# Second score product of the attention at 128 rows, the residual's post-norm weights under an ordering hint, and another buffer for the SGU mix

## The chip, the cores and the metric

One Trainium2 chip, one of its cores. The metric is the time of one execution on the device, in microseconds (us), as the median of several runs. The engines are named as in the profile: PE is the matrix engine (PEld its weight loads), DVE the vector engine, ACT the scalar engine, POOL is GpSimd, SP issues most transfers.

## The reference

Batch 1, 256 latent tokens and 256 context tokens, width 1024, float32. Two "trunk" layers come first, then one block with a forgetting attention, an LRU and a mixture of 32 experts, which the change does not touch. A trunk layer, cut to what matters (the attention has 8 query heads of 64, 2 key heads and 512 keys; layer 0 does the same for the context, over its own 256 keys):

```python
def trunk_layer(x, ctx, c, c_ctx, p, ang_r, ang_c, need_ctx):
    ...
    (a_q, a_k, a_v, a_g, g_q, g_k, g_v, g_af, g_ab, g_g,
     s_u, s_v, s_g, m_a, m_g, m_s) = jnp.split(h @ p['w_in'], pts, axis=-1)
    ...
    y_attn = blocked_attention(ql, k_all, v_all) * jax.nn.silu(a_g)
    ...
    y_gla = gla_finish(ol_f + flip(ol_b), p['gla_o_norm'], x.dtype) * jax.nn.silu(g_g)
    y_sgu = sgu(s_u, s_v, p['sgu_ln_g'], p['sgu_ln_b'], p['sgu_w'], p['sgu_b']) * jax.nn.silu(s_g)
    def merge(ya, yg, ys, ga, gg, gs):
        m = (jax.nn.sigmoid(ga) * (ya @ p['w_br_attn'])
             + jax.nn.sigmoid(gg) * (yg @ p['w_br_gla'])
             + jax.nn.sigmoid(gs) * (ys @ p['w_br_sgu']))
        return m @ p['w_out']
    out = merge(y_attn, y_gla, y_sgu, m_a, m_g, m_s)
    x_new = layer_norm(DEEPNORM_ALPHA * x + gate[:, None, :] * out, p['post_g'], p['post_b'])
    ...
```

## The kernel before, in words

Float32 products are made from a high and a low part of each operand: a product of activations `hTh`, `hTl` with weights `whi`, `wlo` is three matmuls (L228, L229, L230; or L263 to L265). The weights stream from HBM (`raw`), ACT makes the high part (L97) and DVE the low part (L98).

Each trunk layer has three branches that need only its input: attention (`attn_core`), a gated linear attention (GLA, `gla_pair`, two pairs of heads), and the SGU (`sgu_core`). The `merge` then multiplies a gate (`mgps`, three per chunk of columns) with each branch's projection (`brps<-ysg`, `brps<-ygl`, and of the attention) and adds them into `msum`. Layer 0 carries 512 tokens, layer 1 only the 256 latent ones.

The attention takes 128 tokens at a time (`tt`: four in layer 0, two in layer 1). The first two see 512 keys, the last two of layer 0 see 256. For each of four query heads `r` there are two key heads `g`; I call one (`r`, `g`) a head. Its scores are two products into one PSUM tile `asc`: L609 takes all 128 rows (64 rows are the high part of the query, 64 its low part; the high part of the keys, `kh`, stands in both halves of the partitions), and L611 takes 64 rows (the query's high part by the keys' low part `kl`). DVE takes the maximum (L616), ACT the exponential (L619), DVE the sum's reciprocal and the scaling (L620, L621), PE transposes (`trp`, L624), ACT evicts (L626), and PE multiplies by the values into one half of the columns (`aops`, L631). At the end of a `tt`, DVE multiplies by the gate and splits (L635, L637). The SGU multiplies on PE (`mxps`), DVE adds (L917, it empties a PSUM buffer of tag "gm", which the gates `mgps` use too), POOL multiplies (L920), ACT and DVE split (L922).

The order of instructions is not written out: a scheduler at build time walks the program with its own model of the engines and fixes each engine's list. On the chip each engine works through its list in order. A tile's buffer is handed to the next tile of the same tag, which then waits for the old one's readers; the list order follows these waits. `tc.issue_after(i)` adds an ordering edge, without a wait, from instruction `i` to instructions of the same engine.

After layer 1's branches, the residual `x2` (two tiles of 128x1024) is multiplied by a post-norm weight and a bias is added, on POOL (L1132, L1133); the weight comes by a transfer (`post<-post_ln_g`).

Of the kernel before, what the change touches and what calls it, by code (L numbers as in the profile page):

```python
# [10 lines left out]
F32 = mybir.dt.float32  # L11
F32R = mybir.dt.float32r
# [3 lines left out]
OP = mybir.AluOpType  # L16
# [59 lines left out]
class Builder:  # L76
# [409 lines left out]
    def attn_tiles(self):  # L486
        L = self.L
        a1 = self.slot.tile([128, 2, 4, self.nx], F32, tag=self.half, bufs=self.nhalf, name="a1")
        L["a1"] = a1
        L["qT"], L["agT"] = a1[:, 0], a1[:, 1]  # L490

        L["kh"] = self.akv.tile([128, 2, 512], F32R, tag="kh", name="kh")
        L["kl"] = self.akv.tile([128, 512], F32R, tag="kl", name="kl")
        L["v"] = self.akv.tile([128, 4, 128], F32, tag="v", name="v")

    def attn_kv(self, t0, t1):
        nc, a, L = self.nc, self.a, self.L
        kh, kl, v = L["kh"], L["kl"], L["v"]
        tts = range(t0 // 128, t1 // 128)
        g = self.gemm_tok(self.chunk(a["w_in"][self.li], C_AK), tts)  # L500
        for tt in tts:
            kt = self.att.tile([128, 512], F32, tag="att2k", name="ktok")[:, :128]
            nc.scalar.activation(v[:, tt], g[tt][:, 128:256], AF.Copy)
            self.norm_rope(g[tt][:, 0:128], 2, 1, tt, kt.rearrange("p (h e) -> p h e", e=64))
            ps = self.ptr.tile([128, 128], F32, tag="tr", name="trk")
            nc.tensor.transpose(ps, kt, self.ident)
            ts = slice(tt * 128, tt * 128 + 128)
            for h in range(2):
                pr, other = slice(64 * h, 64 * h + 64), slice(64 - 64 * h, 128 - 64 * h)
                nc.scalar.activation(kh[pr, h, ts], ps[pr], AF.Copy)  # L510
                nc.vector.tensor_tensor(kl[pr, ts], ps[pr], kh[pr, h, ts].bitcast(F32), op=OP.subtract)
                nc.gpsimd.tensor_copy(kh[other, h, ts], kh[pr, h, ts])

    def attn_q(self):
        nc, a, L = self.nc, self.a, self.L
        w = a["w_in"][self.li]
        nq = self.nx // 128
        a1, qT = L["a1"], L["qT"]
        qtok = {}
        for c in range(2):  # L520
            g = self.gemm_tok(self.chunk(w, C_AQ + 256 * c), range(nq))
            for tt in range(nq):
                if c == 0:
                    qtok[tt] = a1[:, 1].rearrange("p r t -> p (r t)")[:, 512 * tt:512 * tt + 512].rearrange(
                        "p (r g e) -> p r g e", r=4, g=2)
                self.norm_rope(g[tt], 4, 0, tt, qtok[tt][:, :, c])
        for tt in range(nq):
            ps = self.ptr.tile([128, 4, 128], F32, tag="tr", name="trq")
            for r in range(4):
                nc.tensor.transpose(ps[:, r], qtok[tt][:, r].rearrange("p g e -> p (g e)"), self.ident)  # L530
            nc.scalar.activation(qT[:, :, tt * 128:tt * 128 + 128], ps, AF.Copy)
# [57 lines left out]
    def attn_core(self):  # L589
        nc, L = self.nc, self.L  # L590
        nq = self.nx // 128
        qT, kh, kl, v = L["qT"], L["kh"], L["kl"], L["v"]
        halves = [slice(64 * g, 64 * g + 64) for g in range(2)]
        y = L["y_a"] = self.slot.tile([128, 2, 4, self.nx], F32R, tag="slot", name="yat")
        for tt in range(nq):
            keys = (0, 512) if tt < 2 else (256, 512)
            nk = keys[1] - keys[0]
            nkc = nk // 128
            ops = self.pou.tile([128, 4, 128], F32, tag="ou", name="aops")

            qs = self.att.tile([128, 4, 2, 128], F32R, tag="qs", name="qs")
            for g in range(2):
                src, hi = qT[halves[g], :, tt * 128:tt * 128 + 128], qs[halves[g], :, g]
                nc.scalar.activation(hi, src, AF.Copy)
                nc.vector.tensor_tensor(qs[halves[1 - g], :, g], src, hi.bitcast(F32), op=OP.subtract)
            for r in range(4):
                sc = [self.psc.tile([128, 512], F32, tag="sc", name="asc")[:, :nk] for g in range(2)]
                for g in range(2):
                    nc.tensor.matmul(sc[g], qs[:, r, g], kh[:, g, keys[0]:keys[1]], start=True, stop=False)  # L609
                for g in range(2):  # L610
                    nc.tensor.matmul(sc[g], qs[halves[g], r, g], kl[halves[g], keys[0]:keys[1]], start=False, stop=True)  # L611
                pts = []
                for g in range(2):
                    s = sc[g]
                    st = self.sm.tile([128, 4], F32, tag="ast", name="ast")
                    nc.vector.tensor_reduce(st[:, 0:1], s, axis=AX.X, op=OP.max)  # L616
                    nc.vector.tensor_scalar(st[:, 1:2], st[:, 0:1], -0.125, None, op0=OP.mult)
                    p = self.att.tile([128, 512], F32, tag="att2k", name="p")[:, :nk]
                    nc.scalar.activation(p, s, AF.Exp, scale=0.125, bias=st[:, 1:2], accum_out=st[:, 2:3])  # L619
                    nc.vector.reciprocal(st[:, 3:4], st[:, 2:3])  # L620
                    nc.vector.tensor_scalar(p, p, st[:, 3:4], None, op0=OP.mult)  # L621
                    tp = self.ptr.tile([128, 4, 128], F32, tag="tr", name="trp")
                    for k in range(nkc):
                        nc.tensor.transpose(tp[:, k], p[:, k * 128:k * 128 + 128], self.ident)  # L624
                    pt = self.att.tile([128, 4, 128], F32, tag="pt", bufs=2, name="pt")
                    nc.scalar.activation(pt[:, :nkc], tp[:, :nkc], AF.Copy)  # L626
                    pts.append(pt)

                for k in range(nkc):
                    for g in range(2):  # L630
                        nc.tensor.matmul(ops[halves[g], r], v[:, keys[0] // 128 + k, 64 * g:64 * g + 64], pts[g][:, k],  # L631
                                         start=(k == 0), stop=(k == nkc - 1), skip_group_check=True)
            t = self.tmp.tile([128, 4, 128], F32, tag="tmp", name="yt")
            tc = slice(tt * 128, tt * 128 + 128)
            nc.vector.scalar_tensor_tensor(t, ops, 0.5, L["agT"][:, :, tc], op0=OP.mult, op1=OP.mult)  # L635
            nc.scalar.activation(y[:, 0, :, tc], t, AF.Copy)
            nc.vector.tensor_tensor(y[:, 1, :, tc], t, y[:, 0, :, tc].bitcast(F32), op=OP.subtract)  # L637


    def gla_tiles(self):  # L640
# [266 lines left out]
    def sgu_core(self):  # L907
        nc, L = self.nc, self.L
        y = L["y_s"]
        for tt in range(self.nx // 128):  # L910
            ps = self.pgm.tile([128, 4, 128], F32, tag="gm", name="mxps")
            for g in range(4):
                nc.tensor.matmul(ps[:, g], L["vn"][:, tt, g * 128:g * 128 + 128], L["wsT"][:, g], start=True, stop=True,
                                 skip_group_check=True)
            t = self.att.tile([128, 4, 128], F32, tag="mx", bufs=1, name="mx")
            for g in range(4):
                nc.vector.scalar_tensor_tensor(t[:, g], ps[:, g], L["vT"][:, 28 + g:29 + g], L["sgr"][:, g],  # L917
                                               op0=OP.mult, op1=OP.add)
            tc = slice(tt * 128, tt * 128 + 128)
            nc.gpsimd.tensor_tensor(t, t, L["su"][:, :, tc], op=OP.mult)  # L920
            nc.scalar.activation(y[:, 0, :, tc], t, AF.Copy)
            nc.vector.tensor_tensor(y[:, 1, :, tc], t, y[:, 0, :, tc].bitcast(F32), op=OP.subtract)  # L922
# [101 lines left out]
    def first_block(self):  # L1024
        nc, tc, a = self.nc, self.tc, self.a
        with ExitStack() as st:
# [15 lines left out]
            with ExitStack() as layer:  # L1042
# [47 lines left out]
                with ExitStack() as inner:  # L1090
                    self.merge_pools(inner)
                    self.xp = self.pool("xp", side="right", reuse_waits="tile")
                    x2 = self.xp.tile([128, 2, D], F32, tag="x", bufs=1, name="x2")
# [25 lines left out]
            with ExitStack() as layer:  # L1119
# [6 lines left out]
                with ExitStack() as inner:  # L1126
# [2 lines left out]
                    self.h2T = [h2p.tile([128, 8, 256], F32R, name=n) for n in ("h2Th", "h2Tl")]  # L1129
                    pv = self.post_norm(0)  # L1130
                    for t in range(2):
                        nc.gpsimd.tensor_tensor(x2[:, t], x2[:, t], pv[:, 0], op=OP.mult)  # L1132
                        nc.gpsimd.tensor_tensor(x2[:, t], x2[:, t], pv[:, 1], op=OP.add)  # L1133
                    pv = self.post_norm(1)
                    side = self.pool("lru", side="right", stack=self.right, reuse_waits="tile")
                    self.merge(iter(()))
# [25 lines left out]
                    ps = self.psc.tile([128, 512], F32, tag="sc", name="rmps")  # L1162
# [808 lines left out]
```

## Time and profile before

| | before |
|---|---|
| median of 3 runs | 1340.52 us (1338.68 to 1343.06) |
| the profiled execution | 1342.17 us, span 1339.8 us |
| mean granted PE clock | 0.981 of full speed |
| PE busy | 1262.4 us, 94% of the span |
| DVE, ACT, POOL busy | 724.2, 577.9, 334.9 us |

The span is the profiled stretch on the core; the remaining 2.4 us of the execution lie outside it. Layer 0's attention scores run from 258.6 us on, layer 1's end at 869.4 us. A clock of 1.00 in a row is 2.4 GHz, 0.50 is 1.2 GHz.

### The profile page before, as it was taken

The numbers are of one execution on the slowest core, as the hardware profiler recorded it, in microseconds if no ns is written. First come the engines' busy times: TensorE is split into PE (matmuls) and PEld (weight loads), VectorE is DVE, ScalarE is ACT, GpSimd is POOL, SyncE is SP. The second block draws the span as 40 slices with busy tenths as digits, with TensorE's granted clock in tenths as the row PEclk, the third lists the DMA queues.
The fourth block names the chain that finished last, engine by engine and source line by source line (L and its number), as shares of the span: only waits on it lengthen the run. The fifth ranks groups of instructions, "written<-read, shape, count | busy, mean of one in ns | idle before, by whom it ended". The sixth has DMA issues, their size and how long they took to land.

```text
span 1339.8 us, 22959 instructions
## 1 busy us (share of the span) xinstructions
PE 1262.4 (94%) x8819; PEld 977.2 (73%) x8819; DVE 724.2 (54%) x1428; ACT 577.9 (43%) x1115; POOL 334.9 (25%) x373
## 2 busy tenths in 40 slices
PE   6999999999999999999999999999899989999975
PEld 3789888777777766799989988799898675333311
DVE  2565585775443323378768877646878455111112
ACT  2463454455343222346776554545465333222201
POOL 2237645340001101242246545002124020000000
PEclk9999999999999999999999999999899799999998
DMA  9613222211124676545555546246498546999994
GB/s 320 188 53 110 74 58 79 65 48 48 48 75 132 188 252 221 173 149 167 152 149 157 138 116 186 67 126 193 123 327 252 187 174 257 409 408 409 408 409 185
DMA packets 182165, 243.89 MB, mean 182 GB/s; under 512 B 15284, under 2 KB 154780, under 8 KB 182048
## 3 DMA queue, kind: packets, MB, share of 16 engines
q1 hardware_dynamic: 182048, 242.35, 54.9%
q8 instruction: 71, 1.16, 0.4%
q14 instruction: 46, 0.38, 0.1%
HBM read 241.27 MB, written 1.05 MB: 181 GB/s over the span
## 4 chain that ended last, share of the span: by engine, by line
PE 65%; DMA 15%; DVE 8%; ACT 4%; issue 3%; POOL 2%; SPq 1%; ACTq 0%; DVEq 0%; POOLq 0%
DMA gu<-w_up 7%; PE mgps L228 5%; PE mgps L230 5%; PE mgps L229 5%; PE gmt L263 4%; PE gmt L264 4%; PE gmt L265 4%; PE gups L1737 3%; DVE wlo L98 2%; DMA dn<-w_down 2%; DMA raw<-w_in 2%; PE brps L228 2%; PE brps L229 2%; PE brps L230 2%; PE aops L631 2%
## 5 line engine op out<-in xcount | busy, mean ns | idle before, releaser
L98 DVE TENSOR_TENSOR wlo<-raw,whi 128x1024 fp32r<-128x1024 f32 (+1 forms) x202 | 253.5, 1261 | 156.7 <-ACT whi L97 153.8
L97 ACT ACTIVATE whi<-raw 128x1024 fp32r<-128x1024 f32 (+1 forms) x216 | 212.5, 993 | 199.3 <-PE mgps L229 41.8
L264 PE MATMUL gmt<-wlo,hTh 128*128 128x256 f32 x480 | 138.0, 288 | 2.5 <-DVE wlo L98 2.5
L263 PE MATMUL gmt<-whi,hTh 128*128 128x256 f32 x480 | 137.3, 287 | 2.1 <-DVE a L587 0.9
L265 PE MATMUL gmt<-whi,hTl 128*128 128x256 f32 x480 | 137.3, 286 | 0.0
L228 PE MATMUL mgps<-hTh,whi 128*128 128x512 f32 (+1 forms) x384 | 132.0, 345 | 0.0
L229 PE MATMUL mgps<-hTl,whi 128*128 128x512 f32 (+1 forms) x384 | 130.6, 340 | 0.0
L230 PE MATMUL mgps<-hTh,wlo 128*128 128x512 f32 (+1 forms) x384 | 130.4, 342 | 0.0
L957 POOL TENSOR_TENSOR msum<-msum,tanh 128x512 f32<-128x512 f32 (+1 forms) x32 | 36.8, 1154 | 329.7 <-DVE tanh L956 310.2
L1737 PE MATMUL gups<-gu,xw 128*64 128x512 f32 (+1 forms) x512 | 97.5, 603 | 8.4 <-DMA gu<-w_up 8.4
L264 PEld LDWEIGHTS gmt<-wlo,hTh 128*128 128x128 f32 x480 | 92.6, 193 | 5.9 <-DVE wlo L98 2.9
L263 PEld LDWEIGHTS gmt<-whi,hTh 128*128 128x128 f32 x480 | 92.5, 193 | 3.9 <-ACT g L669 1.1
L265 PEld LDWEIGHTS gmt<-whi,hTl 128*128 128x128 f32 x480 | 92.7, 193 | 2.3 <-issue 2.2
L228 PEld LDWEIGHTS mgps<-hTh,whi 128*128 128x128 f32 x384 | 72.6, 189 | 12.9 <-issue 5.0
L230 PEld LDWEIGHTS mgps<-hTh,wlo 128*128 128x128 f32 x384 | 72.5, 189 | 10.2 <-issue 2.5
L229 PEld LDWEIGHTS mgps<-hTl,whi 128*128 128x128 f32 x384 | 72.7, 189 | 9.0 <-issue 2.0
L1737 PEld LDWEIGHTS gups<-gu,xw 128*64 128x64 f32 (+1 forms) x512 | 25.3, 124 | 62.0 <-issue 60.0
L203 POOL TENSOR_TENSOR frs<-rsq,mhalf 128x1 f32<-128x1 f32 x2 | 1.1, 549 | 234.7 <-DVE frs L1911 234.7
L1769 DVE SCALAR_TENSOR_TENSOR eth<-eth,gups 128x256 f32<-128x256 f32 x12 | 5.1, 421 | 99.8 <-ACT eth L1768 99.8
L1792 PE MATMUL dnps<-dn,hm 128*64 128x512 f32 (+1 forms) x256 | 52.2, 599 | 6.2 <-DMA dn<-w_down 6.0
L264 PE MATMUL gmt<-wlo,mm 128*128 128x256 f32 x192 | 54.5, 285 | 0.6 <-DVE wlo L98 0.6
L263 PE MATMUL gmt<-whi,mm 128*128 128x256 f32 x192 | 54.1, 285 | 0.0
(559 smaller groups left out, 3109.2 us busy)
## 6 DMA issues: line engine op xcount, KB each, us to landing
raw<-w_in SPq DMA_DIRECT2D x132, 512.0 KB
gu<-w_gate SPq DMA_DIRECT2D x64, 512.0 KB
gu<-w_up SPq DMA_DIRECT2D x64, 512.0 KB
dn<-w_down SPq DMA_DIRECT2D x28, 1024.0 KB
adar<-w_ada SPq DMA_DIRECT2D x32, 512.0 KB
raw<-w_out SPq DMA_DIRECT2D x32, 512.0 KB
adaw<-w_ada SPq DMA_DIRECT2D x16, 512.0 KB
raw<-w_in SPq DMA_DIRECT2D x32, 256.0 KB
```

What stands on the lines that cost most here:

```text
L97: nc.scalar.activation(hi, x, AF.Copy)
L98: return (eng or nc.vector).tensor_tensor(lo, x, hi.bitcast(F32), op=OP.subtract).ins
L228: nc.tensor.matmul(ps, wh, xh, start=(u == 0 and k == 0), stop=False)
L229: nc.tensor.matmul(ps, wh, xl, start=False, stop=False)
L230: nc.tensor.matmul(ps, wl, xh, start=False, stop=(u == len(acts) - 1 and k == 3))
L263: nc.tensor.matmul(out[tt], xh, hi[:, j, :n], start=first, stop=False, skip_group_check=True)
L264: nc.tensor.matmul(out[tt], xh, lo[:, j, :n], start=False, stop=False, skip_group_check=True)
L265: nc.tensor.matmul(out[tt], xl, hi[:, j, :n], start=False, stop=last, skip_group_check=True)
L631: nc.tensor.matmul(ops[halves[g], r], v[:, keys[0] // 128 + k, 64 * g:64 * g + 64], pts[g][:, k], start=(k == 0), stop=(k == nkc - 1), ski ...
L957: nc.gpsimd.tensor_tensor(sums[c, j], sums[c, j], ts[j], op=OP.add)
L1737: mm = nc.tensor.matmul(u["ps"][pr], u["x"][:, k, pr], u["gu"][ei][k // 4][:, :, k % 4], start=(k == 0), stop=(k == 7), skip_group_check=T ...
L1792: mm = nc.tensor.matmul(ps[pr], hm[:, f, pr], dns[ei][:, f, 512 * hf:512 * hf + 512], start=(f == 0), stop=(f == 1), skip_group_check=True ...
```

## The change

Three edits. The low part of the keys gets a copy in the other half of the partitions (16 more POOL copies of 64x128 in all), and the second score product then takes all 128 rows, right behind the first, head by head. The four POOL instructions on `x2` come under `issue_after(self.last_y)`, where `last_y` is the DVE instruction L637. The SGU's tile `mx` leaves the attention's pool, where it had a buffer of its own, for the pool and tag "tmp" (three buffers), which `yt` of the attention and `osq` and `on` of the GLA use.

```diff
-        L["kl"] = self.akv.tile([128, 512], F32R, tag="kl", name="kl")
+        L["kl"] = self.akv.tile([128, 2, 512], F32R, tag="kl", name="kl")
...
-                nc.vector.tensor_tensor(kl[pr, ts], ps[pr], kh[pr, h, ts].bitcast(F32), op=OP.subtract)
+                nc.vector.tensor_tensor(kl[pr, h, ts], ps[pr], kh[pr, h, ts].bitcast(F32), op=OP.subtract)
                 nc.gpsimd.tensor_copy(kh[other, h, ts], kh[pr, h, ts])
+                nc.gpsimd.tensor_copy(kl[other, h, ts], kl[pr, h, ts])
...
                 for g in range(2):
-                    nc.tensor.matmul(sc[g], qs[:, r, g], kh[:, g, keys[0]:keys[1]], start=True, stop=False)
-                for g in range(2):
-                    nc.tensor.matmul(sc[g], qs[halves[g], r, g], kl[halves[g], keys[0]:keys[1]], start=False, stop=True)
+                    for kx in (kh, kl):
+                        nc.tensor.matmul(sc[g], qs[:, r, g], kx[:, g, keys[0]:keys[1]], start=(kx is kh), stop=(kx is kl))
...
-            nc.vector.tensor_tensor(y[:, 1, :, tc], t, y[:, 0, :, tc].bitcast(F32), op=OP.subtract)
+            self.last_y = nc.vector.tensor_tensor(y[:, 1, :, tc], t, y[:, 0, :, tc].bitcast(F32), op=OP.subtract).ins
...
-            t = self.att.tile([128, 4, 128], F32, tag="mx", bufs=1, name="mx")
+            t = self.tmp.tile([128, 4, 128], F32, tag="tmp", name="mx")
...
                     for t in range(2):
-                        nc.gpsimd.tensor_tensor(x2[:, t], x2[:, t], pv[:, 0], op=OP.mult)
-                        nc.gpsimd.tensor_tensor(x2[:, t], x2[:, t], pv[:, 1], op=OP.add)
+                        with tc.issue_after(self.last_y):
+                            nc.gpsimd.tensor_tensor(x2[:, t], x2[:, t], pv[:, 0], op=OP.mult)
+                            nc.gpsimd.tensor_tensor(x2[:, t], x2[:, t], pv[:, 1], op=OP.add)
```

With the keys' low part in both halves, the second product also adds the query's low part by the keys' low part, which the reference's exact product contains.

The lists of the engines move. On PE, in layer 1's attention, the list of before has gate products between a head's scores, transposes and value products:

```order
L624 MATMUL trp<-ident,p 128x128 x4
L230 MATMUL mgps<-hTh,wlo 128x256
L228 MATMUL mgps<-hTh,whi 128x256
L229 MATMUL mgps<-hTl,whi 128x256
L631 MATMUL aops<-pt,v 64x128 x7
L609 MATMUL asc<-kh,qs 128x512
L611 MATMUL asc<-kl,qs 128x512
L230 MATMUL mgps<-hTh,wlo 128x256
L624 MATMUL trp<-ident,p 128x128 x4
L228 MATMUL mgps<-hTh,whi 128x256
```

The list of the change has, from the products of GLA pair 1 (`attps`) on, no such work; L611 is now the line of both score products. Its start:

```order
L807 MATMUL attps<-qlv,klv 64x64 x48
L807 MATMUL attps<-qlv,g_6093 64x64 x16
L611 MATMUL asc<-kh,qs 128x512
L611 MATMUL asc<-kl,qs 128x512
L611 MATMUL asc<-kh,qs 128x512
L611 MATMUL asc<-kl,qs 128x512
L829 MATMUL gops<-S,qin 128x128 x4
```

A little further on, where the heads' transposes begin:

```order
L849 MATMUL tro<-ident,on 128x128 x4
L624 MATMUL trp<-ident,p 128x128 x8
L631 MATMUL aops<-pt,v 64x128
L611 MATMUL asc<-kh,qs 128x512
L611 MATMUL asc<-kl,qs 128x512
L631 MATMUL aops<-pt,v 64x128 x7
L624 MATMUL trp<-ident,p 128x128 x4
```

And its end, behind which all gates have moved:

```order
L624 MATMUL trp<-ident,p 128x128 x4
L631 MATMUL aops<-pt,v 64x128 x8
L228 MATMUL mgps<-hTh,whi 128x256
L229 MATMUL mgps<-hTl,whi 128x256
L230 MATMUL mgps<-hTh,wlo 128x256
```

All 64 `attps` of GLA pair 1 now stand without other work between them, and so do the heads of the attention; `tro` (the GLA's output transposes) stands ahead of the first head's transposes. In layer 0 the gates and the branch products of the SGU and the GLA have likewise moved behind the attention.

On DVE, at the end of layer 1's attention, the list of the change has the adds of the SGU's mix behind the attention's last output (before, they stood among the GLA's `qlv` and `accd` rows):

```order
L621 TENSOR_SCALAR p<-p,ast 128x512
L635 SCALAR_TENSOR_TENSOR yt<-aops,a_6095 128x512
L917 SCALAR_TENSOR_TENSOR mx<-mxps,vT,sgr 128x128 x8
L637 TENSOR_TENSOR yat<-yt,yat 128x4x128
L922 TENSOR_TENSOR ysg<-mx,ysg 128x4x128 x2
L98 TENSOR_TENSOR wlo<-raw,whi 128x1024 x2
```

L917 empties the PSUM buffers for which the gates on PE wait. On POOL the four instructions on `x2` (now L1133 and L1134) stand in the list of the change between the GLA's two `on` products, as they did before, and not behind the attention:

```order
L203 TENSOR_TENSOR ors<-rsq,mhalf 128x2
L846 TENSOR_TENSOR on<-on,g_6094 128x256
L1133 TENSOR_TENSOR x_3747<-x_3747,post 128x1024 x2
L203 TENSOR_TENSOR ors<-rsq,mhalf 128x2
L1134 TENSOR_TENSOR x_3747<-x_3747,post 128x1024 x2
L846 TENSOR_TENSOR on<-on,g_6094 128x256
L1169 MEMSET r2T 128x4x3
L920 TENSOR_TENSOR mx<-mx,s_7281 128x512 x2
```

The SGU's multiplications L920 have moved behind them; before, they stood among the GLA's `klv` rows.

## Rows read from the trace of the kernel before

**Rows 1.** The page: busy time; GB/s in 40 slices.
```profile
PE 1262.4 (94%) x8819; PEld 977.2 (73%) x8819; DVE 724.2 (54%) x1428; ACT 577.9 (43%) x1115; POOL 334.9 (25%) x373
...
GB/s 320 188 53 110 74 58 79 65 48 48 48 75 132 188 252 221 173 149 167 152 149 157 138 116 186 67 126 193 123 327 252 187 174 257 409 408 409 408 409 185
```

**Rows 2.** Windows: window, length, busy of each engine (instructions), clock, DMA share, GB/s.
```profile
280.00:300.00 20.00, 17.77 (x123) 12.75 (x123) 17.44 (x46) 12.01 (x26) 5.52 (x4) 1.00 0.17 51
780.00:800.00 20.00, 18.73 (x217) 16.97 (x216) 16.65 (x38) 10.80 (x23) 9.34 (x12) 0.91 0.30 87
810.00:820.00 10.00, 8.38 (x71) 8.18 (x70) 7.02 (x10) 3.16 (x5) 8.26 (x4) 1.00 0.39 121
860.00:870.00 10.00, 10.00 (x77) 7.64 (x76) 5.47 (x12) 6.34 (x13) 0.00 (x0) 1.00 0.34 91
```

**Rows 3.** Timeline of PE at layer 0's scores: start, duration, instruction.
```profile
266.64 0.49 PE L611 MATMUL asc<-kl,qs 64*128 64x512 f32 x2
267.06 0.50 PE L228 MATMUL sgps<-hTh,whi 128*128 128x512 f32 x1
...
302.38 0.39 PE L230 MATMUL mgps<-hTh,wlo 128*128 128x512 f32 x1
302.60 0.40 PE L609 MATMUL asc<-kh,qs 128*128 128x512 f32 x1
302.93 0.50 PE L611 MATMUL asc<-kl,qs 64*128 64x512 f32 x1
303.36 0.87 PE L624 MATMUL trp<-ident,p 128*128 128x128 f32 x6
...
334.39 0.28 PE L609 MATMUL asc<-kh,qs 128*128 128x256 f32 x1
334.91 0.50 PE L228 MATMUL mgps<-hTh,whi 128*128 128x512 f32 x1
335.24 0.40 PE L229 MATMUL mgps<-hTl,whi 128*128 128x512 f32 x1
```

**Rows 4.** All matmuls of line L611: count, duration, first and last start, forms.
```profile
L611 PE MATMUL asc<-kl,qs x48: 379/492/502, 258.6 to 869.4; 64*128 64x512 f32 x32, 64*128 64x256 f32 x16
```

**Rows 5.** Groups by line in layer 1's attention, 798 to 882 us.
```profile
L631 PE MATMUL aops<-pt,v 128*64 128x128 f32 x128 | 12.2, 282 | 0.0
L616 DVE TENSOR_REDUCE ast<-asc 128x1 f32<-128x512 f32 x16 | 11.0, 688 | 8.6 <-PE asc L611 8.6
L619 ACT ACTIVATE p<-asc,ast 128x512 f32<-128x512 f32 x16 | 11.0, 685 | 6.9 <-PE trp L624 4.9 <-DVE ast L617 1.9
L626 ACT ACTIVATE pt<-trp 128x512 f32<-128x512 f32 x16 | 9.5, 596 | 13.3 <-PE trp L624 9.2 <-PE aops L631 4.0
L621 DVE TENSOR_SCALAR p<-p,ast 128x512 f32<-128x512 f32 x16 | 8.9, 555 | 0.7
```

**Rows 6.** The chain of waits in layer 1, 798 to 827 us: start, length, what.
```profile
798.41 0.67 PE attps L807 x31
...
805.75 5.92 DMA post<-post_ln_g
811.74 1.21 POOL x L1132
...
824.49 1.74 POOL on L846
826.27 0.44 PE tro L849 x2
```

**Rows 7.** Timeline of POOL around GLA pair 1: first and last `klv`.
```profile
773.55 0.98 POOL L793 TENSOR_TENSOR klv<-g 128x128 f32<-128x128 f32 x1 [1.56 <-PE trkh L749]
...
789.30 1.53 POOL L796 TENSOR_TENSOR klv<-klv,g 128x256 f32<-128x256 f32 x2
```

**Rows 8.** Group by line, 770 to 882 us: the adds of the SGU's mix.
```profile
L917 DVE SCALAR_TENSOR_TENSOR mx<-mxps,vT,sgr 128x128 f32<-128x128 f32 x8 | 2.2, 340 | 0.7 <-PE mxps L913 0.7
```

**Rows 9.** A window of the second block's attention, columns as in rows 2.
```profile
1050.00:1055.00 5.00, 5.00 (x16) 2.88 (x16) 2.43 (x6) 0.38 (x1) 0.00 (x0) 0.50 0.57 193
```

## The prediction

> **What bounds the kernel now.** I read the page first. PE is busy for 1262.4 of 1339.8 us [rows 1], so I ask of each edit how much PE work it removes and how much PE idle time it makes. The windows then show where PE waits: in layer 1's attention it is busy 10.00 of 10 us in 860:870 [rows 2], because gate products stand between the heads; where this cover is thin, at 280 to 300 us, it is busy 17.77 of 20 us, with DVE at 17.44. At the end the page shows some 409 GB/s for four slices and more [rows 1]: there the expert weights stream as fast as they ever do, into buffers that come free late. No expert load is issued in the trunk layers, so I take it that time lost in them reaches the end one to one.
>
> **The change, part by part.** The sum is made against the profiled execution, 1342.2 us, 1.7 us above the median of 1340.5; I apply the difference to the median.
>
> *The second product with 128 rows.* A pair of scores for 512 keys takes from 302.60 to 303.36, 0.76 us [rows 3]. A full-array product of the same width that follows another takes 0.22 us (302.38 to 302.60). The difference sits where the number of rows changes: 0.33 us from L609 to L611, 0.43 us from L611 to the next, and a full-array product behind 64-row work still takes 0.33 us to its follower (334.91 to 335.24). Two full products would take 0.44 us, so a pair saves 0.32, and some 0.1 more where a full-array product follows; I take 0.40. For 256 keys a pair takes 0.52 us (334.39 to 334.91), against about 2 x 0.11, half of 0.22: 0.30 and the same 0.1, so 0.40 again. There are 48 pairs, 32 of 512 keys and 16 of 256 [rows 4]. In the lists 42 pairs are followed by a full-array product; 6 stand between value products (64 columns, which change the array anyhow), and I give these 0.2. So 42 x 0.40 + 6 x 0.2 = 18 us of PE work less; bounds 16 and 20.
>
> The Trainium skill's page "TensorEngine Tiling (Array Packing)", section Key Properties, says that switching the tiling mode drains the engine, and that different tiles run in parallel. The first agrees with the 0.33 and 0.43 above. The second speaks against the edit, and where two 64-row products stand together the trace agrees: both take 0.42 us, from 266.64 to 267.06 [rows 3]. By that rule alone the edit would gain only the switches; since the list of before has the two side by side at one place of the 24, the sum would not be different by more than 0.5 us.
>
> The 16 more POOL copies lie below the 0.98 us of a `klv` copy, which moves twice their size [rows 7]: at most 16 us, I take half, on an engine that is busy a quarter of the time [rows 1]. They stand among the projections, whose PE work hides them until the first scores. I cost them at nothing; without that cover the last of them would delay each layer's first score by 1 us.
>
> *The mix in the pool "tmp".* This is the edit that I cost highest. The SGU's tile now takes its turn with the attention's `yt`, so its adds L917 stand behind the last attention output in DVE's list, in both layers. They free the PSUM buffers for which the gates wait, so every gate and the SGU's and GLA's branch products stand behind the attention on PE. The work is the same; the cover is gone. Four places lose it.
>
> Layer 0's attention: a head of 512 keys has PE work of some 1.7 us (0.44 for scores, 4 transposes at 0.87/6 = 0.145 [rows 3], 4 value products at 12.2/128 = 0.095 [rows 5], 0.3 for two changes to and from 64 columns, priced as those of the scores), DVE 0.69 + 0.56 and two small instructions, ACT 0.69 + 0.60 and one small one [rows 5], say 1.5 us each. Three engines at nearly the same load, each in order: I take 1.85 us a head, and 1.25 for 256 keys with 0.95 of PE work. That is 16 x 0.15 + 16 x 0.3 = 7 to 8 us. The upper bound takes 2.4 us for the long heads, half as much again as one engine's work, and 11 us more in all. Behind the last head its chain (max, exponential, scaling, transposes, eviction, values: 3 us) and L635 and the mixes, eight L917 at 0.34 [rows 8] and what they wait for in turn, come before the gates: 8.5 us in all, 3 for the chain, the rest estimated. Less 2.2 us that is idle there already (20 - 17.77 [rows 2]). Sum +14; bounds 4 and 25.
>
> GLA pair 1 of layer 1: the 64 `attps` wait for POOL's `klv`, which run from 773.55 to 790.83 [rows 7], and reach PE up to 798.41 [rows 6]. Before, gates fill this: PE idles 1.3 us in 780:800 [rows 2]. Without them, and with the two POOL mixes gone from between the `klv`, I count 16 us with 4 us of PE work, so 12 idle, less 1.7: +10; bounds 4 and 12.
>
> The residual on POOL: in the built list, the four instructions on `x2` stand between the GLA's two `on` products, as before; the ordering edge goes from a DVE instruction and reaches none on POOL. So they wait for the transfer `post`, 5.92 us behind the last `gops`, from 805.75 on; POOL then works through `x2` and `on` until 826.23, and `tro` starts at 826.27 [rows 6]. Before, gates and branch products fill that (8.38 of 10 us in 810:820 [rows 2]). Now only two heads' scores stand ahead of `tro`, and behind `tro` all transposes of the heads wait. One `on` now comes ahead of `x2`, so `tro` may start at the same time or 1.7 us sooner. 20.5 us, less 1.7 and some 3 us of PE work, are 15.5 us of idle time, less the 1.9 of before (1.6 of them in that window): +13.5; bounds 11 and 16. This costs what the GLA's output waits for, not what the residual needs.
>
> Layer 1's attention: 16 heads of 512 keys at 0.15 to 0.3 us each, the first head's filling (2 us), the last head's chain (3 us) and L635 and L917 until the first gate (2.1 us): +10.5; bounds 5 and, at 2.4 us a head, 18.
>
> *The clock.* In 780:800 the granted clock is 0.91 [rows 2]: it fell to 1.2 GHz for about 3.5 us behind a PE wait, and half of that, 1.8 us, is lost. In the second block's unfilled attention it stays at 0.50 for a whole window [rows 9]. Three of the new waits (the GLA, the residual, a drain) are longer than those; at 1.8 us each that is +5; bounds 2 and 9.
>
> The sum: -18 + 14 + 10 + 13.5 + 10.5 + 5 = +35 us. From the median, 1340.5 + 35 = **1375 us**. With all low bounds -20 + 4 + 4 + 11 + 5 + 2 = +6 (1346), with all high ones -16 + 25 + 12 + 16 + 18 + 9 = +64 (1404).
>
> **The rivals.** *The cover was worth little, and the change is faster.* At 280 to 300 us, thinly filled, PE loses 2.2 of 20 us [rows 2]. If the unfilled stretches (layer 0's heads 50 us, the GLA 16, the residual 19, layer 1's heads 30: 115 us) lost no more than that rate, they would cost 13 us against 18 gained: 1340.5 - 5 = 1335. It decides where the added idle time is below 18 us. For it: that stretch has real PE work from the attention. Against it: the POOL row up to 824.49 + 1.74, whose order the change leaves as it was, alone leaves over 13 us.
>
> *The clock stays low through the attention.* As in the second block [rows 9], PE works at 1.2 GHz while its work is full of short waits. A head's PE work would be 3.3 us instead of 1.7, above DVE's and ACT's, so layer 1's 16 heads would take 16 x (3.3 - 1.85) = 23 us more: 1398. Against it: at 280 to 300 us the clock was 1.00 in spite of the waits.
>
> *The loss is absorbed behind the trunk.* If transfers of the second block, now with more time, land ahead of their use, some 20 of the 35 us come back: 1355. Against it: the streams at 409 GB/s start from buffers that come free late.
>
> *The wait does not do what it says.* It does not, by the lists; that is in the sum. Had POOL put `x2` behind the attention, the 13.5 us would be gone: 1361.
>
> **How the numbers follow.** My forecast (1355 to 1392) has 0.58, the low clock 0.13, absorption or several low bounds (1345 to 1355) 0.11, no change 0.05, the faster rival 0.13. What a measurement of this kernel can tell from no change is about 0.3%, 4 us: 1336.5 to 1344.5. So faster 0.13, same 0.05, slower 0.82. The range that leaves 2 in 10 out reaches from 1344 to 1402.
>
> **What would show it.** Right: the PE row of scores has 96 products of full height, with 0.22 us slots behind one another; layer 1 has a PE wait of some 15 us that ends with POOL's `on` and `tro`; the chain of waits holds `post` and the `x2` rows; no gate lies between the heads, and behind each attention stands a PE wait that ends with L917. Wrong: PE busy above 90% of each window of both attentions, or `tro` of layer 1 less than 10 us behind the last `gops`; or the heads' pace above 2.5 us, which would be the low clock if the granted clock there is 0.50.

## The result, and the profile of the changed kernel

The change makes the kernel slower: a median of 1357.22 us over 4 runs (1351.13 to 1360.16), against 1339.60 us for the kernel before over its 4 runs. The ratio is 1.0138, with a 95% interval of 1.0108 to 1.0167: +18 us, between +14 and +22. I had forecast +35 us, 1375, with 1344 to 1402 as the range. A second set of 6 runs gave 1.0154 (1.0119 to 1.0189).

The page of the changed kernel, against [rows 1]; the last two rows are the tenths of PE's clock and the GB/s in 40 slices of 33.9 us:

```profile
span 1355.0 us, 23023 instructions
PE 1257.8 (93%) x8819; PEld 980.2 (72%) x8819; DVE 718.6 (53%) x1428; ACT 579.0 (43%) x1115; POOL 340.5 (25%) x389
...
PEclk9999999999999999999999959999999899999988
...
GB/s 332 175 68 91 83 63 79 63 32 43 85 94 109 202 252 213 140 175 154 156 171 133 148 63 1 172 181 180 154 247 330 127 199 254 410 408 409 408 409 186
```

PE has the same number of instructions and is busy 4.6 us less, but the span is 15.2 us longer, so nearly 20 us of PE wait were added. The clock has one slice at half (the 24th, 779 to 813 us), and the streams behind the trunk are as fast as before.

The scores do what was meant. The timeline of PE, layer 0 (start, duration, instruction):

```profile
254.27 0.39 PE L229 MATMUL sgps<-hTl,whi 128*128 128x512 f32 x1
254.50 0.40 PE L611 MATMUL asc<-kh,qs 128*128 128x512 f32 x1
254.73 0.39 PE L611 MATMUL asc<-kl,qs 128*128 128x512 f32 x1
254.96 0.40 PE L230 MATMUL sgps<-hTh,wlo 128*128 128x512 f32 x1
```

A pair takes 0.46 us from start to start, and the work behind it follows as if nothing had been between; in [rows 3] the pair took 0.76.

Where the time went shows in windows of the changed kernel (columns as in rows 2). First layer 0's attention and its end, then in layer 1: GLA pair 1, its outputs, the wait for the residual, the attention, its end.

```profile
278.00:328.00 50.00, 45.80 (x342) 30.87 (x340) 38.63 (x125) 34.08 (x95) 0.30 (x1) 1.00 0.03 10
328.00:335.00 7.00, 2.52 (x19) 2.05 (x18) 6.64 (x18) 1.89 (x3) 2.53 (x3) 1.00 0.62 188
335.00:350.00 15.00, 15.00 (x57) 10.98 (x58) 5.57 (x10) 5.13 (x9) 2.87 (x2) 0.89 0.15 38
...
770.00:787.00 17.00, 10.59 (x184) 8.68 (x183) 13.37 (x35) 8.65 (x27) 11.53 (x19) 0.77 0.26 75
787.00:794.00 7.00, 7.00 (x30) 5.39 (x31) 3.74 (x12) 3.16 (x8) 0.00 (x0) 0.50 0.00 0
794.00:808.00 14.00, 1.94 (x6) 0.72 (x5) 3.22 (x10) 0.38 (x1) 12.01 (x8) 0.50 0.23 75
808.00:811.00 3.00, 2.92 (x12) 2.11 (x12) 0.59 (x2) 1.84 (x5) 0.00 (x0) 0.50 0.92 300
811.00:840.00 29.00, 27.86 (x222) 20.13 (x221) 18.65 (x54) 18.47 (x44) 0.11 (x1) 0.96 0.02 6
840.00:843.00 3.00, 1.18 (x14) 0.94 (x11) 2.49 (x9) 0.63 (x1) 0.62 (x1) 1.00 0.00 0
```

The kernel before, in the windows nearest to these (layer 0's thin stretch, then layer 1: GLA, residual, attention):

```profile
281.00:297.00 16.00, 13.77 (x96) 9.39 (x96) 13.86 (x35) 10.08 (x22) 5.08 (x4) 1.00 0.15 51
758.00:800.00 42.00, 40.23 (x416) 37.07 (x415) 31.86 (x69) 24.03 (x55) 23.52 (x30) 0.96 0.44 126
800.00:830.00 30.00, 28.09 (x218) 25.39 (x217) 21.38 (x35) 13.75 (x26) 15.17 (x8) 1.00 0.53 158
830.00:882.00 52.00, 52.00 (x394) 41.37 (x393) 30.80 (x66) 26.91 (x54) 4.57 (x7) 1.00 0.35 102
```

The reader is to see three things: PE idles 6.4 of 17 us in the GLA and 12.1 of 14 us ahead of the residual's end; the attention itself, unfilled, idles only 1.1 of 29 us; and all of 787 to 811 us runs at 1.2 GHz. The chain of waits names the long wait (start, length, what), to be held against [rows 6]:

```profile
793.60 3.66 DMA post<-post_ln_g
797.33 1.50 POOL x L1133
798.83 0.79 issue
799.62 2.34 POOL x L1133
801.96 0.66 POOL ors L203
802.62 0.51 POOL x L1134
803.13 1.76 issue
804.89 2.33 POOL x L1134
807.23 0.69 POOL on L846
807.96 0.70 PE tro L849 x2
```

It is the wait that the gates had covered before: `tro` 14.4 us behind the last GLA output instead of 20.5, since the transfer lands sooner (3.66 us instead of 5.92), one `on` now runs ahead of `x2`, and POOL's rows on `x2` and `on` are shorter here. Measured from landmarks in the two traces, the first score comes 3.8 us earlier (L609 at 258.27, L611 now at 254.50; 258.6 was the first row of the old L611), layer 0's merge ends 1.6 us earlier, and layer 1's merge ends 16 us later; nothing of this comes back before the end of the span.

### The profile page after: what moved, and what is told of

Same layout as the page of the kernel before. It is cut to its first block, busy times and chain, and to the rows that moved or that the text cites. A ratio compares the mean times of both kernels' runs of the same rounds, so it can differ in the third digit from the quotient of the medians.

```text
span 1355.0 us, 23023 instructions
## 1 busy us (share of the span) xinstructions
PE 1257.8 (93%) x8819; PEld 980.2 (72%) x8819; DVE 718.6 (53%) x1428; ACT 579.0 (43%) x1115; POOL 340.5 (25%) x389
## 4 chain that ended last, share of the span: by engine, by line
PE 62%; DMA 17%; DVE 8%; ACT 5%; POOL 3%; issue 3%; SPq 1%; ACTq 0%; DVEq 0%; POOLq 0%
DMA gu<-w_up 10%; PE mgps L228 5%; PE mgps L229 5%; PE mgps L230 5%; PE gmt L263 5%; PE gmt L264 5%; PE gmt L265 5%; DMA dn<-w_down 3%; PE brps L228 2%; PE brps L229 2%; PE brps L230 2%; DVE wlo L98 2%; PE aops L631 2%; PE asc L611 1%; DMA raw<-w_in 1%
## 5 line engine op out<-in xcount | busy, mean ns | idle before, releaser
L98 DVE TENSOR_TENSOR wlo<-raw,whi 128x1024 fp32r<-128x1024 f32 (+1 forms) x202 | 245.7, 1221 | 200.1 <-ACT whi L97 198.8
```

The lines of the kernel that those rows point to most:

```text
L98: return (eng or nc.vector).tensor_tensor(lo, x, hi.bitcast(F32), op=OP.subtract).ins
```

## The experiments

All ratios are to runs of the kernel before beside them on the same chip; 1% is 13.4 us. With the larger low part of the keys there is no room any more for the mix's own 2 KB buffer in the attention's pool, so the mix was put, where it should take no turn in a pool, into the buffer of its own input, which no one reads after it.

**The change with the mix in the buffer of its input.**

```diff
-            t = self.tmp.tile([128, 4, 128], F32, tag="tmp", name="mx")
+            t = L["vn"][:, tt].rearrange("p (g n) -> p g n", n=128)
```

> 128-row products, but the SGU's mix in the buffer of its own input, so that it takes no turn in the pool tmp; the built lists have gates between the heads again. Theory 1 (the products save 18 us of PE time and the lost cover costs about 36): 1322 us, ratio to before 0.987 (0.983 to 0.991). Rival (the products save nothing on the path, the lost cover alone makes the whole loss of 18): 1340 us, ratio 1.000.

Measured: 1314.96 us, 0.9820 (0.9797 to 0.9843), 24 us faster than before. The windows of its trace show the cover restored:

```profile
280.00:300.00 20.00, 20.00 (x120) 15.97 (x119) 15.91 (x38) 11.38 (x22) 5.52 (x4) 1.00 0.13 39
780.00:800.00 20.00, 19.30 (x173) 17.46 (x172) 16.55 (x28) 10.13 (x18) 7.52 (x5) 1.00 0.51 153
```

The rival, that the products save nothing on the path, falls. But 24 us are more than theory 1 gave, and the control below says why.

**The control: the kernel before with the mix in that place, nothing else** (the same two lines in the kernel before).

> A control: the kernel before with the mix in the buffer of its input and nothing else. If the place of the mix matters only by its turn in a pool, this is the kernel before: ratio 1.000 (0.996 to 1.004). If two mixes at a time instead of one already fill the attention better, up to 4 us less than before, and that part of the gain of the first experiment is not the products'.

Measured: 1331.09 us, 0.9945 (0.9926 to 0.9963), 7 us faster. So 7 of the 24 us belong to the place of the mix, a little more than I allowed. The products, copies included, are 0.9820 against 0.9945: -16.7 us. The thin stretch of [rows 2] is one place where the 7 us come from; PE is now busy 19.67 us in it:

```profile
280.00:300.00 20.00, 19.67 (x121) 15.12 (x121) 15.81 (x38) 10.25 (x22) 6.96 (x5) 1.00 0.12 37
```

**The kernel before with the mix in the pool "tmp", nothing else.**

```diff
-            t = self.att.tile([128, 4, 128], F32, tag="mx", bufs=1, name="mx")
+            t = self.tmp.tile([128, 4, 128], F32, tag="tmp", name="mx")
```

> The kernel before with one edit alone, the mix in the pool tmp; 64-row products as before. Theory 1: 1340 + 36 = 1376 us, ratio 1.027 (1.020 to 1.034). Rival (the products save nothing): the same as the change, 1357 us, ratio 1.013.

Measured: 1376.26 us, 1.0270 (1.0233 to 1.0307): +36 us for this line alone. The change as a whole costs 18 to 21, so the products take 15 to 18 us off here too. The lost cover looks as in the change, with the clock at half for longer (a window over the end of layer 0's attention and the first gates, then two ahead of and in layer 1's residual wait):

```profile
318.30:355.80 37.50, 34.07 (x122) 22.61 (x123) 20.65 (x67) 13.42 (x41) 5.37 (x4) 0.50 0.13 38
806.00:816.00 10.00, 9.59 (x44) 6.12 (x36) 5.23 (x16) 3.15 (x8) 0.69 (x1) 0.50 0.09 29
816.00:834.00 18.00, 6.92 (x27) 4.08 (x29) 6.52 (x14) 3.23 (x8) 11.30 (x7) 0.50 0.29 101
```

In layer 0 the clock is at half while PE is busy for 34.1 us; just before, from 300 to 318 us, PE was busy 17.28 of 18 us at full clock. The change has only 3.4 us of such work in layer 0. Half of the 31 us between them, an estimated 15 us, is clock, so in these two traces, 24 us apart, the clock makes up most of what the products seem to take off here. Their price is better read where both kernels are covered, from the control: -16.7 us.

**The pool "tmp" in one layer only.** The mix takes the turn in `tmp` in one layer and stands in the buffer of its input in the other (the diff is that for layer 0; the other run has 1 in its place).

```diff
-            t = self.tmp.tile([128, 4, 128], F32, tag="tmp", name="mx")
+            t = (self.tmp.tile([128, 4, 128], F32, tag="tmp", name="mx") if self.li == 0
+                 else L["vn"][:, tt].rearrange("p (g n) -> p g n", n=128))
```

In layer 0:

> The change, with the mix in the pool tmp in layer 0 alone (in layer 1 in the buffer of its input). Theory 1, with my sizes of layer 0 (14 us and a part of the clock): 1322 + 15 = 1337 us, ratio 0.998 (0.994 to 1.002). Rival (only layer 1 loses, layer 0's attention is filled well enough by itself): 1322 us, ratio 0.987.

Measured: 1331.78 us, 0.9942 (0.9920 to 0.9965). Against the first experiment that is +16 us for layer 0. The traces of the first experiment and of this run, from the first score to the last product of layer 0's merge:

```profile
254.90:599.70 344.80, 343.37 (x2089) 270.66 (x2088) 170.25 (x335) 133.53 (x227) 62.67 (x40) 1.00 0.45 137
258.30:621.20 362.90, 351.39 (x2089) 274.55 (x2088) 169.22 (x335) 133.47 (x227) 60.37 (x40) 1.00 0.43 130
```

Of the 18 us, 10 are idle time of PE, and for 8 us PE is busy longer with as many products. In layer 1:

> The change, with the mix in the pool tmp in layer 1 alone. Theory 1, by the PE idle time that the trace of the change shows more in layer 1 (18 us) and the clock at half (6 us): 1322 + 24 = 1346 us, ratio 1.004 (0.999 to 1.009). By my sum before the run, with 34 us of idle time there: 1322 + 37 = 1359 us, ratio 1.014. Rival (layer 0 makes the loss): 1322 to 1327 us.

Measured: 1339.25 us, 0.9996 (0.9978 to 1.0014): +23.5 us for layer 1. The two add up to 40, and the change stands 43 to 45 (1.0138 or 1.0154 against 0.9820) above the first experiment. Both layers pay, and the pre-run sum of layer 1 (1359) was too high by 20; the count from the idle time and the clock of the trace (1346) came nearer.

**The residual really behind the GLA's outputs.** In the change, the hint names a DVE instruction. With and without it the scheduler writes the same lists for all engines, instruction by instruction, so the hint does nothing. Here it names the POOL instruction of the GLA's second `on`:

```diff
-            nc.gpsimd.tensor_tensor(on, on, L["gg"][:, :nch, hd * 128:hd * 128 + 128], op=OP.mult)
+            self.last_on = nc.gpsimd.tensor_tensor(on, on, L["gg"][:, :nch, hd * 128:hd * 128 + 128], op=OP.mult).ins
...
-                        with tc.issue_after(self.last_y):
+                        with tc.issue_after(self.last_on):
```

> The change, with the four residual instructions put behind the GLA's second product on GpSimd by a hint on an instruction of GpSimd itself. Theory 1 (tro waits for the residual, which waits for the weight's transfer): the 11 us of PE wait before tro go, and with them part of the half clock: 1357 - 12 = 1345 us, ratio 1.004 (1.001 to 1.007). Rival (the attention behind it is paced by its own chain, the wait is only moved to its end): 1357 us, ratio 1.013.

Measured: 1348.62 us, 1.0068 (1.0043 to 1.0094). The change, run again beside it:

> The change itself beside the two above on one chip: ratio 1.014 by all theories (1.011 to 1.017).

Measured: 1358.64 us, 1.0154 (1.0119 to 1.0189). So the wait was worth 11.5 us. The chain of waits in this kernel goes from `gops` over `on` to `tro` without `post` and `x2`:

```profile
796.12 0.43 PE gops L833 x2
...
797.69 0.71 POOL ors L203
798.42 0.42 DVE on L845
798.93 0.73 POOL on L846
799.70 0.45 PE tro L849 x2
...
801.49 0.73 POOL on L846
802.27 0.70 PE tro L849 x2
```

The second `tro` comes 5.7 us behind the last `gops` instead of 14.4 (793.60 to 807.96 in the change).

**Both: mix in the buffer of its input, residual behind the outputs** (the two edits above together).

> The first experiment (mix in the buffer of its input, 128-row products) with the residual put behind the GLA's second product as well. Theory 1: the wait before tro is filled by gates there, so that the hint is worth 0 to 3 us: 1320 us, ratio 0.985 (0.981 to 0.989). Rival (the wait holds up the attention also where it is filled): 1310 us, ratio 0.978.

Measured: 1311.21 us, 0.9778 (0.9749 to 0.9807), the fastest of all: 30 us faster than before (2.2%) and some 47 faster than the change. The hint is worth 5.6 us here (0.9778 against 0.9820), though the intervals overlap; it lies between my 0 to 3 and the rival's 12, and the ratio is the one that the rival gave only because the first experiment was faster than forecast. What the 5.6 us are is open: from layer 1's first GLA product (`attps`) to the end of its merge PE idles 3.0 us here and 3.1 in the first experiment, so no PE wait went. What differs in the two traces is the clock: the first experiment has three stretches of 3.4 us at half before 930 us (10 us of PE work, an estimated 5 us lost), this kernel none, and two of the three lie far ahead of the hint's place.

**The two 64-row products side by side.** On the control, a hint makes the low products of both heads wait in the list for the second high product.

```diff
                 for g in range(2):
-                    nc.tensor.matmul(sc[g], qs[:, r, g], kh[:, g, keys[0]:keys[1]], start=True, stop=False)
+                    m = nc.tensor.matmul(sc[g], qs[:, r, g], kh[:, g, keys[0]:keys[1]], start=True, stop=False)
                 for g in range(2):
-                    nc.tensor.matmul(sc[g], qs[halves[g], r, g], kl[halves[g], keys[0]:keys[1]], start=False, stop=True)
+                    with self.tc.issue_after(m.ins):
+                        m = nc.tensor.matmul(sc[g], qs[halves[g], r, g], kl[halves[g], keys[0]:keys[1]], start=False, stop=True)
```

> The control (the kernel before with the mix in the buffer of its input, 64-row products), with a hint that puts the two 64-row products of a pair of heads side by side on PE, in all 24 places instead of one. If the gain of the 128-row product is the changes of row number that it saves, half of the changes go here too and the two halves overlap: 1.18 us (0.65 + 0.42 + 0.11) instead of 2 x 0.86 for a pair of heads of 512 keys, so some 16 x 0.54 + 8 x 0.4 = 12 us less than the control, 1319 us, ratio to before 0.985 (0.982 to 0.989). Rival (the gain comes from the order that the second product right behind the first allows, the softmax starts earlier): nothing or a loss against the control, ratio 0.994 or more.

Measured: 1318.30 us, 0.9861 (0.9834 to 0.9888), 11 us less than the control, as the count gave (half of the row changes and the overlap of the halves together; the run does not part them). In the traces the two stand side by side in 23 of the 24 places, and in 4 in the control, not in all 24 and in one. Its timeline (L612 is the low product here):

```profile
265.79 0.40 PE L609 MATMUL asc<-kh,qs 128*128 128x512 f32 x1
266.11 0.49 PE L612 MATMUL asc<-kl,qs 64*128 64x512 f32 x2
266.54 0.50 PE L229 MATMUL sgps<-hTl,whi 128*128 128x512 f32 x1
266.87 0.40 PE L230 MATMUL sgps<-hTh,wlo 128*128 128x512 f32 x1
```

Two products of 64 rows take 0.43 us, from 266.11 to 266.54, which is what one took before. That agrees with the Trainium skill, "TensorEngine Tiling (Array Packing)", Key Properties, which says that different tiles can execute matmuls in parallel. The edit gets two thirds of the products' gain with no copies and no larger tile.

**The new copies twice**, on the first experiment.

```diff
                 nc.gpsimd.tensor_copy(kl[other, h, ts], kl[pr, h, ts])
+                nc.gpsimd.tensor_copy(kl[other, h, ts], kl[pr, h, ts])
```

> The first experiment (128-row products, mix in the buffer of its input) with each of the 16 new GpSimd copies of the keys' low part made twice. If the copies are hidden by the projections: as the first experiment, ratio to before 0.982 (0.979 to 0.986). Rival (GpSimd delays the scores): up to 16 x 0.4 = 6 us more, ratio 0.986 or more, and the change's own copies would have cost the same.

Measured: 1323.89 us, 0.9904 (0.9876 to 0.9933): +11 us, against my expectation. 16 more copies of 0.29 us are 4.7 us of POOL time, so most of it must come in another way. PE's windows in layer 1:

```profile
690.00:706.00 16.00, 12.10 (x100) 11.69 (x99) 12.85 (x24) 8.79 (x19) 15.17 (x23) 1.00 0.51 136
800.00:820.00 20.00, 14.46 (x100) 13.17 (x100) 10.32 (x17) 7.98 (x14) 15.44 (x9) 0.83 0.51 159
```

Without the second copies the same windows have PE busy 14.48 and 18.57 us, POOL 15.13 and 9.07. The scheduler also wrote another list for PE. So two more runs take the copies from POOL altogether, on the fastest kernel:

```diff
-                nc.gpsimd.tensor_copy(kl[other, h, ts], kl[pr, h, ts])
+                nc.vector.tensor_tensor(kl[other, h, ts], ps[pr], kh[pr, h, ts].bitcast(F32), op=OP.subtract)
```

> The kernel with the mix in the buffer of its input and the residual behind the GLA's second product, with the other half of the keys' low part written by a second subtraction on DVE instead of a copy on GpSimd. Theory (layer 1's rotation of the queries waits for GpSimd, and the copies stand ahead of it): 2 to 8 us less than with the copies, ratio to before 0.972 to 0.977. Rival (the 11 us of the doubled copies come from other lists that the scheduler made, not from GpSimd's time): as with the copies, 0.978 within 0.002.

Measured: 1311.65 us, 0.9813 (0.9783 to 0.9843). And with `nc.scalar.activation(kl[other, h, ts], kl[pr, h, ts].bitcast(F32), AF.Copy)` in its place:

> The same with the copies on ACT. ACT is busy 8.6 of 14 us in layer 1's rotation, GpSimd 13.1: theory as with DVE, 2 to 8 us less, ratio 0.972 to 0.977; rival 0.978 within 0.002. If the two runs fall on different sides, the lists decide and not the engine's time.

Measured: 1312.22 us, 0.9824 (0.9785 to 0.9864). Neither is below the 0.9778 with the copies on POOL; both lie a little above the rival's 0.978 within 0.002 as well. The theory that the copies themselves cost time on the path falls for this kernel; what made the doubled copies cost 11 us (other lists, or POOL's lateness carried to the wait before `tro`, which the fastest kernel no longer has) is not told apart.

## Why the prediction was right, and where its sizes were off

The direction and the mechanism were right, and the time lay in the range. The point was 18 us too high: +35 forecast, +18 measured. The runs add up: the first experiment's -24, +16 for layer 0 and +23.5 for layer 1 give +16, against +18 and +21 measured. One of my own signs of being wrong did show: PE is busy 92% of the heads' window in layer 0 (45.80 of 50) and 96% in layer 1 (27.86 of 29). The heads themselves lose little; the loss sits at the ends, in the GLA, ahead of `tro` and in the clock. Step by step:

- **The products, -18 us**: measured -16.7 (first experiment against the control) and 15 to 18 (the change against the mix alone, where the clock has a large part). The count carried: the side-by-side run took 11 us where 12 were counted. Right.
- **The mix in "tmp" moves every gate behind the attention**: right, and it is the whole loss. The step that failed is its size: +53 us over its five terms, where that line alone costs +36.
- **Layer 0, +14**: measured +16 against the mix in its input's buffer; that the sum came so near is luck. Its idle time was smaller: 4.2 us in the heads (50.00 - 45.80) and 4.5 in the end (7.00 - 2.52), less the 2.2 of before: +6.5 (10 against the first experiment, which is covered better than before). A cost that I had put at nothing, with PE's work taken as the same with and without cover, made up for it: against the first experiment PE is busy 8 us longer with the same products, of which an estimated 1.7 are the clock in 335:350. I also read a transpose as 0.145 us off a merged row (0.87/6), whose length holds the end of its last one; from start to start one behind another takes 0.11 us.
- **GLA pair 1, +10**: 6.4 us of idle time in 770:787, less 1.7: +4.7. I counted 16 us with 4 us of PE work. The window has 10.59 us of it, in part at half clock, and POOL's `klv` take 12 us (771.10 to 783.22) instead of 17.3; part of the waits that are left end with `qlv` on DVE and ACT.
- **The residual's wait, +13.5**: 12.1 us less 1.9, +10.2 by the windows, and 11.5 by the experiment that removes it. Right in place, somewhat smaller since the transfer and POOL were faster than in [rows 6].
- **Layer 1's attention, +10.5**: 1.1 + 1.8, some +3. The heads go at the pace that I took (3.76 us a pair of heads, from 813.89 to 817.65), but PE is busy in nearly all of it; the filling fell into the residual's wait, and of the last head's chain only L635 and L917 stayed open. This is the largest of the errors.
- **The clock, +5**: it is at half from 779.1 to 813.3 us, with 18 us of PE work, and for 3.4 us in 335:350. Half of that work, an estimated 9 and 1.7 us, less the 1.8 of before, makes some +9. Larger than I took, but not the same in each execution: the trace of the repeat has it at half from 783.5 to 793.7 and from 800.6 to 814.2 us, with 10.6 us of PE work.
- **The copies, nothing**: no cost was found by taking them from POOL, though doubling them cost 11 us; open, as said.
- **Not named**: the lists of the change also differ ahead of the scores. In layer 0's first GLA pair PE waits less (160 to 180 us: busy 19.66 us, before 17.68), and the first score comes 4 us earlier (2 us in the repeat's trace). That alone is a gain that no edit was meant to bring.

Of the rivals, the faster one failed on its own condition: the unfilled stretches did lose little PE time in the attention, as it said, but not in the GLA and ahead of `tro`; the added idle time, nearly 20 us, lies just above the 18 at which it would have held. The clock did fall to half, though in the GLA and the wait; the attention's heads run at 1.00 from 813.3 us on. The row that I gave for the low clock's rival does not show work full of short waits: PE is busy all 5.00 us of it [rows 9]. What comes nearest to this rival is the kernel before with the mix in "tmp" alone, whose layer 0 has 37.5 us at half. Nothing was absorbed behind the trunk.

## What to carry to other kernels

A buffer that a tile shares with a later stage is an ordering edge: before moving a tile into a shared pool to win space, look at what it will wait for and what waits behind it, here all gates behind a PSUM buffer. A dead input is often a free place for a result. A hint orders only the engine of the instruction that it names, so look in the built lists whether it moved anything. And in a sum of waits do not add each stage's chain whole: where two stages overlap, only the last of them stays open.

## What the runs showed that I had not expected

The same products cost PE more time where nothing stands between them. Counted from each start to the next without PE's idle time, a transpose goes from 112 to 146 ns in layer 0's attention (10.8 and 14.0 us over 96), and the 192 value products from 17.3 to 19.4 us. In part that only moves the cost to other rows: 20 transposes instead of 4 now stand right ahead of a value product of 64 columns, at some 0.23 us each, where before gates stood and took 0.33 instead of 0.23; a transpose ahead of another takes 0.11 us in the median of both traces, and layer 0's gates and branch products together take 3.4 us less. Why the rest costs more was not tested. And the place of one 2 KB tile is worth 7 us by itself in the kernel before, nearly half of the gain of the products. Runs of one kernel spread by 1% and more (1323 to 1337 us for one of them, 1365 to 1383 for another), so the last two kernels and the fastest, 0.35% and 0.46% apart with intervals of 0.3 to 0.4% to each side, are not told apart here.
